# Early pairs of a SwiGLU: the weight sum a21 + a22 from two transfers on GpSimd's queue instead of a VectorE addition

## The chip, the cores and the metric

The kernel runs on one core of one Trainium2 chip. The metric is the device time of one execution in microseconds, the median of several runs.

## The reference

Two token groups (512 and 256 tokens, 768 together, width 1024) go through a two-layer encoder with shared weights. Each layer is a half SwiGLU, a mixer, and another half SwiGLU, so there are four SwiGLUs in all:

```
def swiglu(h, wg, wu, wd):
    return (jax.nn.silu(h @ wg) * (h @ wu)) @ wd

x = x + 0.5 * swiglu(rmsnorm(x, f1_n), f1_g, f1_u, f1_d)
x = x + mixer(rmsnorm(x, mix_n), ...)
x = x + 0.5 * swiglu(rmsnorm(x, f2_n), f2_g, f2_u, f2_d)
```

The hidden width is 2816, all data are float32. The mixer of the first layer is a spatial gating unit beside windowed attention; that of the second is neighbourhood attention. A last RMSNorm follows.

## The kernel before

**Arithmetic.** A float32 product is made of three products of rounded operands: each operand is split into a rounded part and a remainder (`wsplit`, lines 112 to 124: ScalarE casts the weights to `whi`, line 122, and VectorE subtracts to get `wlo`, line 123), and TensorE multiplies hi x hi, lo x hi and hi x lo (`mm3`, line 188).

**Seven products for eight.** The hidden width is cut into 11 pairs of 128-column tiles. In one pair, the weights of gate (and likewise of up) are a 2 x 2 matrix of blocks of 512 x 128: a11 and a12 (first tile, upper and lower half of the 1024 rows), a21 and a22 (second tile). The activations are cut in two halves of 384 tokens and two halves of the width. Each 2 x 2 block product is done by Winograd's scheme with seven block products in place of eight. They need weight combinations, made by `sums` (line 725) into tiles of 128 x 512 in the work pool (tag "s", a ring of eight):

- s1 = a21 + a22 (for the product with activations t1)
- s2 = s1 - a11 (for t2)
- s3 = a11 - a21 (for t3)
- s4 = a12 - s2 (for b22), in place of s2

All of these are VectorE instructions on line 727. A weight tile of 128 columns and 1024 rows is one transfer of 512 KB by SyncE's queue (`raw`, line 99) into a ring of four buffers.

**Early pairs.** The first four pairs of each SwiGLU (`EARLY`) run in two parts. First, in an order written out by hand (`ORDERS`, line 699; twelve steps, three per pair), only the products with b11 and b21 and the first hidden quarter are made; they need just a11 and a12, and the other activations are not ready yet. Later each of the four pairs loads its two tiles again (`entry`, line 641) and makes the other five products for gate and up, ten in all (`settle`, line 645), in the order t2, t3, n4, t1, b22. In `settle` the weights of the next product are prepared by `parts` (line 546) while the current one runs; the t2 weights of the next pair's gate are prepared at the end of the current pair, for pairs 1 and 2. While a pair settles, VectorE also makes the operands for the down projection of the pair before (`operands`, line 492). After pair 2 the down projection of pairs 0 and 1 runs (`down`, line 747), and so on for each two pairs.

**Order.** TensorE's order is as the program emits it. The other engines' order is made ahead by the framework's scheduler, which may bring instructions forward, transfers above all, when their buffers are free; on the chip each queue then runs strictly in order. In the second and fourth SwiGLU, those after a mixer, GpSimd makes the remainders `wlo` of the b11 weights of pairs 1 to 3; otherwise it has nothing to do near the early pairs.

`raw` has one more duty: from the 20th weight transfer on, each call also issues one small copy that builds tables for the second mixer on SyncE's queue (`spare`).

Of the kernel before, what the change touches and what calls it, by code (L numbers as in the profile page):

```python
# [9 lines left out]
F32 = mybir.dt.float32  # L10
# [4 lines left out]
ALU = mybir.AluOpType  # L15

P = 128
D = 1024
KD = D // P
FF = 2816  # L20
# [24 lines left out]
EARLY = 4  # L45
ORDERS = (0, 1, 0, 1, 2, 2, 0, 1, 3, 2, 3, 3), (0, 1, 0, 1, 0, 2, 1, 3, 2, 3, 2, 3)

WTOTAL = 12 * D * FF + 8 * EARLY * P * D + D * 1792 + 2 * D * D + D * 3072 + D * 512
VTOK = (4.0,9.0)
GAP0 = 5.2  # L50
SGU = (8.0, 3.0, 4.0)
# [4 lines left out]
class Trunk:  # L56
# [39 lines left out]
        return side  # L96


    def raw(self, name, k0, nk, c0, n, raw=None, eng=None):
        i = len(self.units)  # L100
        self.units.append((name, k0, nk, c0, n))
        size = P * nk * n
        src = self.aps["w"][self.woff : self.woff + size].rearrange("(p f) -> p f", p=P)
        self.woff += size
        if raw is None:
            raw = self.rawp.tile([P, nk * n], F32, tag="raw", name=f"raw{i}")
        (eng or self.nc.sync).dma_start(raw, src)
        if self.spare and i >= 20:
            self.spare.pop(0)()
        return raw.rearrange("p (k n) -> p k n", k=nk)  # L110
# [367 lines left out]
    def ffn(self, pre):  # L478
        nc = self.nc
# [3 lines left out]
        mixed = bool(self.unfed)  # L483
# [37 lines left out]
            yield sub(h21, h21, h11)  # L521
            yield put("n4", h21)

        entries, entered = {}, {}

        def pair(p):

# [2 lines left out]
            names = ("gate", "up")  # L530
            a = {}

            def load(tiles):
                for n in names:
                    for i in tiles:
                        r = self.first.pop(0) if self.first else self.raw(f"{pre}_w_{n}", 0, KD, (2 * p + i) * P, P)
                        a[n, i + 1, 1], a[n, i + 1, 2] = r[:, 0:4, :], r[:, 4:8, :]

            h = hs[p] = {}
            s, bank, e = {}, {}, {}  # L540
# [5 lines left out]
            def parts(n, b):  # L546
                name = {"t2": "s2", "t3": "s3", "t1": "s1", "b22": "s4"}.get(b)
                with self.tc.high_priority() if b == "t2" and p == urgent else nullcontext():
                    return self.wsplit(sums(n, name) if name else a[n, 2, 2], nc.vector)

            def product(n, w, b, key, start, st=None):
                if start:
                    mm = key == "Y" or key == "X" and p != EARLY - (1 if mixed else 2)
                    bank[key, n] = (self.psum() if mm else self.psum(self.aux, "aux"))[:, :H]
                self.run_until(lambda: b in self.made)
                with ExitStack() as stack:
                    if early and b in ("b11", "b21"):
                        stack.enter_context(self.tc.high_priority())
                    if early and not fresh and b in ("b11", "b21"):
                        if len(order) >= NW and order[-NW]:  # L560
                            stack.enter_context(self.tc.issue_after(order[-NW]))
                        order.append(None)
                    st = st or self.wsplit(w, nc.gpsimd if early and mixed and p and b == "b11" else nc.vector)
                for k in range(4):
                    self.mm3(
                        bank[key, n], (st[0][:, k, :], st[1][:, k, :]), self.b[b][k], start and k == 0, k == 3, not start
                    )

            def keep(out, key, n):

                e[n, out] = etile(out)
                nc.scalar.copy(e[n, out], bank[key, n])  # L572
                next(steps, None)
# [6 lines left out]
            def hidden(i, half, g, u):  # L580

                self.run_until(lambda: half in scales)
                h[i, half] = t = g if half else etile("sg")
                v = u if half else etile("v")
                r = rt[:, HALVES[half][0] : HALVES[half][1]]
                nc.vector.tensor_tensor(out=t, in0=g, in1=r, op=ALU.mult)  # L586
                nc.scalar.activation(t, t, AF.Silu)
                self.freed = nc.vector.tensor_tensor(out=v, in0=u, in1=r, op=ALU.mult).ins
                nc.vector.scalar_tensor_tensor(out=t, in0=t, scalar=0.5, in1=v, op0=ALU.mult, op1=ALU.mult)  # L589

            def begin(n, p1):

                bank["Y", n] = self.psum()[:, :H]
                nc.scalar.copy(bank["Y", n], p1)
# [40 lines left out]
            def p3():  # L635
# [2 lines left out]
                    add("Z", n, "u2")  # L638
                hidden(0, 1, e["gate", "u2"], e["up", "u2"])

            def entry():
                load((0, 1))
                return parts("gate", "t2")

            def settle(st):

                todo = [(n, b) for b in ("t2", "t3", "n4", "t1", "b22") for n in names]
                key = {"t1": "Z", "b22": "Z"}
                for i, (n, b) in enumerate(todo):
                    now, st = st, None  # L650
                    if i + 1 < len(todo):
                        st = parts(*todo[i + 1])
                    elif p + 1 < EARLY and (p % 2 or not p):
                        entered[p + 1] = entries[p + 1]()
                    if b == "t2":
                        begin(n, e[n, "p1"])
                    product(n, None, b, key.get(b, "Y"), b == "t1", now)
                    if b in ("t2", "t3"):
                        keep(b.replace("t", "u"), "Y", n)
                    elif b == "n4":  # L660
                        next(steps, None)
                    else:
                        add("Z", n, "u3" if b == "t1" else "u2")
                    if n == "up":
                        if b == "n4":
                            hidden(1, 0, bank["Y", "gate"], bank["Y", "up"])
                        elif b == "t1":
                            hidden(1, 1, e["gate", "u3"], e["up", "u3"])
                        elif b == "b22":
                            hidden(0, 1, e["gate", "u2"], e["up", "u2"])  # L670

            if early:
                entries[p] = entry
                load((0,))
                p1()
                yield
                p2()
                yield
                with self.tc.high_priority():
                    hidden(0, 0, bank["X", "gate"], bank["X", "up"])  # L680
                self.hids.append(self.freed)
                yield
# [5 lines left out]
                steps = operands(p - 1) if p < NPAIR - 1 else self.last_operands(dl, 0, hs[p - 1], acc)  # L688

            if early:  # L690
                settle(now)
            else:
                for f in (p1, p6, p2, p7, p4, p5, p3) if p == NPAIR - 1 else (p1, p6, p2, p7, p5, p3, p4):
                    f()
            for _ in steps:
                pass

        stages = [pair(p) for p in range(NPAIR)]
        for p in ORDERS[mixed]:
            next(stages[p])  # L700
        for p in range(NPAIR):
            for _ in stages[p]:
                pass
            if p == 2:
                acc += [self.fw.tile([P, H], F32, tag=f"p1{j}", name=f"p1{j}") for j in range(4)]
            if p and p % 2 == 0 and p < NPAIR - 1:
                self.down(pre, range(p - 2, p), d, acc)
            if p == NPAIR - 2:
                self.down(pre, range(p - 1, p), d, acc)
# [15 lines left out]
    def sums(self, a11, a12, a21, a22, s, n, name):  # L725

        f = lambda o, x, y, op: self.nc.vector.tensor_tensor(out=o, in0=x, in1=y, op=op)  # L727
        if name == "s1":
            return s[n, "s1"]
        if name == "s4":  # L730
            t = s[n, "s2"]
            f(t, a12, t, ALU.subtract)
            return t
        if name == "s2":
            t = s[n, "s1"] = self.fw.tile([P, 4, P], F32, tag="s", name="s1", bufs=8)
            f(t, a21, a22, ALU.add)
        t = s[n, name] = self.fw.tile([P, 4, P], F32, tag="s", name=name, bufs=8)
        if name == "s3":
            f(t, a11, a21, ALU.subtract)
        else:  # L740
            f(t, s[n, "s1"], a11, ALU.subtract)
        return t
# [989 lines left out]
def trace(nc, phases=PHASES):  # L1732
# [4 lines left out]
    inp("xt", (T // P, P, D))  # L1737
    inp("w", (WTOTAL,))
    inp("gains", (P, KD * len(NORMS)))
# [18 lines left out]
def layout(units, i):  # L1758
    x = np.concatenate([i["x_prompt"][0], i["x_sample"][0]], axis=0)
    w = np.zeros(WTOTAL, np.float32)  # L1760
    off = 0
# [44 lines left out]
```

## Time and profile before

| | us |
|---|---|
| median of 3 runs | 2600.09 (2599.57 to 2600.18) |
| span of the profiled execution | 2599.3 |
| TensorE busy in it | 2557.6 |
| VectorE busy | 2250.6 |
| ScalarE busy | 1364.7 |
| GpSimd busy | 113.4 |

The four SwiGLUs lie at about 0 to 500, 720 to 1240, 1240 to 1740 and 2050 to 2600 us; their early pairs take roughly the first 150 us of each. The table's busy times are sums over the whole span. TensorE's row has the same share nearly everywhere, so the places where it falls short have to be looked for in the timeline. In a timeline row the first number is the start, the second the duration; a bracket at its end gives the idle time of that engine just before the instruction and what ended it.

### The profile page before, as it was taken

The numbers are of one execution on the slowest core, as the hardware profiler recorded it, in microseconds if no ns is written. First come the engines' busy times: TensorE is split into PE (matmuls) and PEld (weight loads), VectorE is DVE, ScalarE is ACT, GpSimd is POOL, SyncE is SP. The second block draws the span as 40 slices with busy tenths as digits, with TensorE's granted clock in tenths as the row PEclk, the third lists the DMA queues.
The fourth block names the chain that finished last, engine by engine and source line by source line (L and its number), as shares of the span: only waits on it lengthen the run. The fifth ranks groups of instructions, "written<-read, shape, count | busy, mean of one in ns | idle before, by whom it ended". The sixth has DMA issues, their size and how long they took to land.

```text
span 2599.3 us, 41191 instructions
## 1 busy us (share of the span) xinstructions
PE 2557.6 (98%) x15114; PEld 2489.5 (96%) x15114; DVE 2250.6 (87%) x4691; ACT 1364.7 (53%) x2869; POOL 113.4 (4%) x191
## 2 busy tenths in 40 slices
PE   8999999999999999999999999999999999999998
PEld 8999999988899999999999999998898999999997
DVE  7998898889779989889999889886777699888897
ACT  7554454556656544445655445454545475444543
POOL 0000000000120000000000000001222210000000
PEclk9999999999999999999999999999999999999999
DMA  6333222421133322223222222242221332222222
GB/s 217 112 106 101 71 82 66 139 84 51 55 106 98 98 66 74 74 65 98 84 95 79 68 76 71 65 145 64 64 64 40 106 98 90 82 68 79 69 67 77
DMA packets 86202, 221.88 MB, mean 85 GB/s; under 512 B 20464, under 2 KB 33264, under 8 KB 86000
## 3 DMA queue, kind: packets, MB, share of 16 engines
q1 hardware_dynamic: 85712, 218.96, 26.9%
q8 instruction: 119, 1.95, 0.3%
q14 instruction: 83, 0.68, 0.1%
q10 hardware_dynamic: 288, 0.29, 0.0%
HBM read 209.78 MB, written 15.07 MB: 87 GB/s over the span
## 4 chain that ended last, share of the span: by engine, by line
PE 66%; DVE 5%; ACT 1%; issue 1%; DMA 1%; DVEq 0%; ACTq 0%; SPq 0%
PE ps_mm L152 40%; PE ps_aux L152 25%; PE ps_aux L156 1%; DVE wlo L123 1%; DMA raw<-in_w 1%; ACT p L1089 0%; DVE tmp L415 0%; DVE p L1099 0%; DVE p L1083 0%; DVE s L727 0%; DMA mf<-in_nmask 0%; DVE u L589 0%; DVE u L577 0%; DVE acc L235 0%; DVE tmp L393 0%
## 5 line engine op out<-in xcount | busy, mean ns | idle before, releaser
L122 ACT CAST whi<-s 128x512 fp32r<-128x512 f32 x496 | 304.9, 621 | 404.7 <-DVE s L727 178.6
L122 ACT CAST whi<-raw 128x512 fp32r<-128x512 f32 x504 | 305.4, 619 | 215.6 <-PE ps_mm L152 87.5
L123 DVE TENSOR_TENSOR wlo<-s,whi 128x512 fp32r<-128x512 f32 x496 | 338.3, 686 | 53.3 <-ACT whi L122 48.2
L123 DVE TENSOR_TENSOR wlo<-raw,whi 128x512 fp32r<-128x512 f32 x468 | 320.7, 693 | 15.2 <-ACT whi L122 11.3
L152 PE MATMUL ps_mm<-db,whi 128*128 128x384 f32 x864 | 219.3, 334 | 0.4 <-DVE sg L586 0.4
L152 PE MATMUL ps_aux<-dt,whi 128*128 128x384 f32 x864 | 219.2, 334 | 0.0
L152 PEld LDWEIGHTS ps_mm<-db,whi 128*128 128x128 f32 x864 | 155.9, 188 | 0.8 <-DVE sg L586 0.8
L152 PEld LDWEIGHTS ps_aux<-dt,whi 128*128 128x128 f32 x864 | 156.0, 188 | 0.0
L152 PE MATMUL ps_mm<-xh,whi 128*128 128x512 f32 (+1 forms) x416 | 146.2, 352 | 0.0
L152 PE MATMUL ps_aux<-dt,wlo 128*128 128x384 f32 x432 | 144.4, 334 | 1.4 <-DVE wlo L123 1.4
L152 PE MATMUL ps_mm<-db,wlo 128*128 128x384 f32 x432 | 144.3, 334 | 0.0
L152 PE MATMUL ps_mm<-xl,whi 128*128 128x512 f32 (+1 forms) x416 | 141.4, 340 | 0.0
L152 PE MATMUL ps_mm<-xh,wlo 128*128 128x512 f32 (+1 forms) x416 | 141.2, 339 | 0.0
L727 DVE TENSOR_TENSOR s<-raw 128x512 f32<-128x512 f32 x124 | 85.0, 687 | 20.9 <-DMA raw<-in_w 20.9
L577 DVE TENSOR_TENSOR u<-ps_aux,u 128x384 f32<-128x384 f32 x176 | 97.3, 553 | 5.6 <-PE ps_aux L152 5.2
L727 DVE TENSOR_TENSOR s<-raw,raw 128x512 f32<-128x512 f32 x124 | 84.2, 687 | 20.4 <-DMA raw<-in_w 20.2
L152 PE MATMUL ps_aux<-dh,whi 128*128 128x384 f32 x384 | 97.5, 334 | 0.0
L779 DVE TENSOR_TENSOR x<-ps_aux,x 128x384 f32<-128x384 f32 x160 | 84.9, 552 | 13.6 <-PE ps_aux L152 13.6
L1089 ACT ACTIVATE p<-p,st 128x256 f32<-128x256 f32 (+3 forms) x144 | 68.9, 480 | 49.4 <-DVE st L1087 49.3
L572 ACT COPY u<-ps_mm 128x384 f32<-128x384 f32 x176 | 83.5, 475 | 16.7 <-PE ps_mm L152 16.6
L779 DVE TENSOR_TENSOR x<-ps_mm,x 128x384 f32<-128x384 f32 x160 | 86.4, 552 | 5.8 <-PE ps_mm L152 5.5
L152 PEld LDWEIGHTS ps_mm<-xh,whi 128*128 128x128 f32 x416 | 79.8, 192 | 9.3 <-issue 0.9
(515 smaller groups left out, 8088.5 us busy)
## 6 DMA issues: line engine op xcount, KB each, us to landing
raw<-in_w SPq DMA_DIRECT2D x346, 512.0 KB, 3.7
xdm<-x SPq DMA_DIRECT2D x16, 384.0 KB, 2.4
x<-in_x SPq DMA_DIRECT2D x16, 192.0 KB, 4.6
tok<-in_xt SPq DMA_DIRECT2D x12, 256.0 KB, 5.2
xold<-xdm SPq DMA_DIRECT2D x8, 384.0 KB, 3.1
x<-xdm SPq DMA_DIRECT2D x8, 384.0 KB, 4.6
out_y<-y SPq DMA_DIRECT2D x8, 384.0 KB, 2.7
tab<-skew SPq DMA_DIRECT2D x8, 256.0 KB, 6.3
```

The lines of the kernel that those rows point to most:

```text
L122: nc.scalar.copy(hi, src)
L123: (eng or nc.gpsimd).tensor_tensor(out=lo, in0=src, in1=hi.bitcast(F32), op=ALU.subtract)
L152: self.nc.tensor.matmul(out, lhsT=lhsT, rhs=rhs, start=start, stop=stop, **kw)
L156: self.nc.tensor.transpose(out, src, self.ident)
L572: nc.scalar.copy(e[n, out], bank[key, n])
L577: nc.vector.tensor_tensor(out=t, in0=bank[key, n], in1=t, op=ALU.add)
L727: f = lambda o, x, y, op: self.nc.vector.tensor_tensor(out=o, in0=x, in1=y, op=op)
L779: nc.vector.tensor_tensor(out=o, in0=ps, in1=o, op=ALU.add)
L1089: ins = nc.scalar.activation(outs[i], outs[i], AF.Exp, bias=nm[:, i : i + 1], accum_out=sm[:, i : i + 1])
```

## The change

In the early pairs, s1 = a21 + a22 is no longer an addition on VectorE. A new function `added` of a pair, for gate and for up, issues two transfers of 256 KB from memory by GpSimd's queue into the s1 tile: a22 plainly, then a21 with an adding write onto it. For that the two blocks are laid out twice more in the weight array, which grows by 4 x 4 x 4 blocks of 256 KB (16.8 MB). `added` of pair 0 is called after the ninth of the twelve early steps; that of pair p + 1 at the start of the settling of pair p. `sums` then makes s2 alone for these pairs. The raw tiles are loaded as before, since s3, s4 and n4 need a21 and a22 as well. The later seven pairs and the down projection are as before.

```diff
-WTOTAL = 12 * D * FF + 8 * EARLY * P * D + D * 1792 + 2 * D * D + D * 3072 + D * 512
+WTOTAL = 12 * D * FF + 16 * EARLY * P * D + D * 1792 + 2 * D * D + D * 3072 + D * 512
...
-    def raw(self, name, k0, nk, c0, n, raw=None, eng=None):
+    def raw(self, name, k0, nk, c0, n, raw=None, eng=None, **kw):
...
-        (eng or self.nc.sync).dma_start(raw, src)
+        (eng or self.nc.sync).dma_start(raw, src, **kw)
...
+            def added():
+                for n in names:
+                    t = s[n, "s1"] = self.fw.tile([P, 4, P], F32, tag="s", name="s1", bufs=8)
+                    for k, kw in ((4, {}), (0, {"accum_op": ALU.add})):
+                        self.raw(f"{pre}_w_{n}", k, 4, (2 * p + 1) * P, P, t.rearrange("p a b -> p (a b)"), nc.gpsimd, **kw)
...
             if early:
-                entries[p] = entry
+                entries[p], addeds[p] = entry, added
...
             if early:
+                if p + 1 < EARLY:
+                    addeds[p + 1]()
                 settle(now)
...
-        for p in ORDERS[mixed]:
+        for i, p in enumerate(ORDERS[mixed]):
             next(stages[p])
+            if i == 8:
+                addeds[0]()
...
+        if name == "s2" and (n, "s1") in s:
+            t = s[n, "s2"] = self.fw.tile([P, 4, P], F32, tag="s", name="s2", bufs=8)
+            f(t, s[n, "s1"], a11, ALU.subtract)
+            return t
```

More of the change, by code (lines that the diff above doesn't have):

```diff
@@ L522, in operands_2 @@
             yield put("n4", h21)
-        entries, entered = {}, {}
+        entries, entered, addeds = {}, {}, {}
         def pair(p):
```

## The prediction

> **What bounds the kernel now.** I read the page first: its engine row and its groups for what the change removes.
>
> ```profile
> PE 2557.6 (98%) x15114; PEld 2489.5 (96%) x15114; DVE 2250.6 (87%) x4691; ACT 1364.7 (53%) x2869; POOL 113.4 (4%) x191
> L727 DVE TENSOR_TENSOR s<-raw 128x512 f32<-128x512 f32 x124 | 85.0, 687 | 20.9 <-DMA raw<-in_w 20.9
> q1 hardware_dynamic: 85712, 218.96, 26.9%
> q10 hardware_dynamic: 288, 0.29, 0.0%
> ```
>
> TensorE (PE) is busy 98% of 2599.3 us, so a faster VectorE (DVE) pays only where PE stands still. The second row is the instruction in question, a21 + a22, 124 times; the change drops 32 of them (4 SwiGLUs, 4 early pairs, gate and up). No queue of GpSimd (POOL) appears: q1 and q10 are SP's and ACT's.
>
> Next the busy time by stretches: two early pairs of the second SwiGLU, what follows them, and one stretch of the third SwiGLU's early pairs.
>
> ```profile
> 804.50:827.40 22.90, 21.85 (x123) 21.00 (x123) 22.67 (x49) 11.87 (x25) 0.00 (x0) 1.00 0.28 92
> 827.40:849.80 22.40, 21.39 (x121) 20.75 (x121) 22.29 (x43) 11.75 (x25) 0.00 (x0) 1.00 0.28 95
> 849.80:900.00 50.20, 50.20 (x290) 50.20 (x291) 45.89 (x84) 25.32 (x51) 0.00 (x0) 1.00 0.30 95
> 1300.00:1320.00 20.00, 20.00 (x116) 20.00 (x117) 19.27 (x35) 10.52 (x21) 0.00 (x0) 1.00 0.37 125
> ```
>
> The columns are length, then PE, PEld, DVE, ACT and POOL busy, granted clock, DMA share and GB/s. In the first two DVE is busy all but 0.23 and 0.11 us, and PE misses about 1 us of each. From 849.8 on PE misses nothing. In the third SwiGLU PE misses nothing even among the early pairs, so relief there is worth nothing.
>
> Then PE's timeline, for every idle piece in the early pairs of the first and second SwiGLU, and the first and the last of six in the fourth (idle 0.95, 0.33, 0.25, 0.79, 0.21, 0.79: a copy of the second).
>
> ```profile
> 54.99 0.45 PE L152 MATMUL ps_mm<-t30h,whi 128*128 128x384 f32 x1 [2.23 <-ACT whi L122]
> 56.28 0.44 PE L152 MATMUL ps_mm<-t30h,wlo 128*128 128x384 f32 x1 [0.68 <-DVE wlo L123]
> 78.73 0.44 PE L152 MATMUL ps_mm<-t20h,whi 128*128 128x384 f32 x1 [1.88 <-ACT whi L122]
> 79.69 0.44 PE L152 MATMUL ps_mm<-t20h,wlo 128*128 128x384 f32 x1 [0.36 <-DVE wlo L123]
> 103.31 0.44 PE L152 MATMUL ps_mm<-t20h,wlo 128*128 128x384 f32 x1 [0.79 <-DVE wlo L123]
> 154.18 0.44 PE L152 MATMUL ps_mm<-t20h,wlo 128*128 128x384 f32 x1 [0.45 <-DVE wlo L123]
> 803.46 0.44 PE L152 MATMUL ps_mm<-t20h,whi 128*128 128x384 f32 x1 [0.95 <-ACT whi L122]
> 804.42 0.45 PE L152 MATMUL ps_mm<-t20h,wlo 128*128 128x384 f32 x1 [0.34 <-DVE wlo L123]
> 807.04 0.44 PE L152 MATMUL ps_mm<-t30h,wlo 128*128 128x384 f32 x1 [0.26 <-DVE wlo L123]
> 827.34 0.45 PE L152 MATMUL ps_mm<-t20h,wlo 128*128 128x384 f32 x1 [0.79 <-DVE wlo L123]
> 848.28 0.44 PE L152 MATMUL ps_mm<-t20h,whi 128*128 128x384 f32 x1 [0.21 <-ACT whi L122]
> 849.70 0.44 PE L152 MATMUL ps_mm<-t20h,wlo 128*128 128x384 f32 x1 [0.80 <-DVE wlo L123]
> ...
> 2130.59 0.45 PE L152 MATMUL ps_mm<-t20h,whi 128*128 128x384 f32 x1 [0.95 <-ACT whi L122]
> ...
> 2176.84 0.44 PE L152 MATMUL ps_mm<-t20h,wlo 128*128 128x384 f32 x1 [0.79 <-DVE wlo L123]
> ```
>
> Nearly all stand before t2, whose weight is s2 = a21 + a22 - a11: the sum, the difference, ACT's rounding (whi), the rest (wlo). Idle sums: 6.39 us in the first SwiGLU, 3.35 in the second, 3.32 in the fourth. Two in the first cost more:
>
> ```profile
> 56.00:64.00 8.00, 7.71 (x35) 7.72 (x36) 6.70 (x18) 4.13 (x10) 0.00 (x0) 0.79 0.39 128
> 78.00:86.00 8.00, 6.92 (x29) 6.61 (x30) 7.49 (x13) 4.49 (x9) 0.00 (x0) 0.79 0.27 70
> ```
>
> After the stops of 2.23 and 1.88 us the granted clock is 0.79 over 8 us, or 0.21 x 8 = 1.7 us lost each time; after the stops under 1 us of the later SwiGLUs it stays at 1.00 (rows above).
>
> **What goes.** DVE's timeline around the stall at 803-804, and three rows for later use:
>
> ```profile
> 800.25 0.69 DVE L727 TENSOR_TENSOR s<-raw 128x512 f32<-128x512 f32 x1
> 800.86 0.16 DVE L327 TENSOR_TENSOR sm<-sm 128x3 f32<-128x3 f32 x1
> ...
> 801.99 0.69 DVE L727 TENSOR_TENSOR s<-s,raw 128x512 f32<-128x512 f32 x1
> ...
> 74.80 0.56 DVE L577 TENSOR_TENSOR u<-ps_aux,u 128x384 f32<-128x384 f32 x1 [0.29 <-PE ps_aux L152]
> ...
> 76.21 0.68 DVE L727 TENSOR_TENSOR s<-raw 128x512 f32<-128x512 f32 x1
> ...
> 824.46 0.68 DVE L727 TENSOR_TENSOR s<-s,raw 128x512 f32<-128x512 f32 x1
> ```
>
> The sum takes 0.69 us but the next instruction starts 0.61 us later, so two sums per pair free 1.2 us of DVE. Where DVE is full, everything behind comes 1.2 us earlier, up to the stall. Second SwiGLU: pair 0 of 1.55 us: 1.2; pair 1: 0.79, all; pair 2: 1.01, all: 3.0. Fourth: 1.2 + 0.79 + 1.0 = 3.0. First: pair 0 of 2.91: 1.2; pair 1 of 2.24: 1.2 (2.24 at most, since its second sum stands late in DVE's order, at 76.21); pair 2: 0.79; pair 3: 0.45: 3.6. Of the two half-clock stretches I count one as gone, 1.7 (none to two, 0 to 3.4), since both stops shrink to about 1 us. Third: 0. Together 11.3 us. What is late next is the same chain without its first link, with DVE still nearly full; the residue (0.35 in the second, 1.7 and 1.0 in the first) stays.
>
> **What comes.** Per early pair four transfers of 256 KB on POOL's queue. No row shows POOL issuing one, nor an accumulating one. Nearest rows:
>
> ```profile
> raw<-in_w SPq DMA_DIRECT2D x8, 256.0 KB, 3.4
> first<-in_w SPq DMA_DIRECT2D x7, 256.0 KB, 5.0
> 59.33 0.34 SPq L107 DMA_DIRECT2D raw<-in_w  x1
> 782.88 1.30 POOL L123 TENSOR_TENSOR wlo<-raw,whi 128x512 fp32r<-128x512 f32 x1 [2.09 <-ACT whi L122]
> L123 POOL TENSOR_TENSOR wlo<-raw,whi 128x512 fp32r<-128x512 f32 x36 | 48.7, 1361 | 833.2 <-ACT whi L122 826.1 <-DVE st L1083 5.2 <-PE ps_mm L152 1.9
> ```
>
> Landing of a plain one: 3.4 us (5.0 in the full start). Accumulating: from 3.4 to four times that, 13.6 us; I take 5, near the plain row, for one more read. Issue: between SP's 0.34 and a POOL pass over such a tile, 1.30; I take 0.8. The accumulate must wait for the plain one, and POOL waits in order, so gate plain, gate accumulating, up plain, up accumulating end 3.4 + 3.4 + 5 + 4 x 0.8 = 15 us after the start. The Trainium skill (DMA: Bandwidth & Descriptors, Two DMAs through the same engine are not ordered) asks for just that wait on the first one's semaphore; no run here shows it yet.
>
> For pairs 1 to 3 the lead is about a pair, over 22 us: hidden, with 7 us to spare. For pair 0 POOL is free at 782.88 + 1.30 = 784.2, so the up sum is there at 799 against the 800.9 at which DVE now has it; if issued at 1.3 it is 801. In the fourth SwiGLU the same. I take off one of the two pair-0 gains, 1.2 (from 0 to 2.4). What is queued behind POOL's waits: its remainders of b11 if transfers slip between them; the last is that row, so I cost that at 0.
>
> The start of the kernel is where added bytes hurt:
>
> ```profile
> 25.00:30.00 5.00, 4.46 (x25) 4.46 (x26) 2.53 (x10) 5.00 (x15) 0.00 (x0) 1.00 1.03 402
> ...
> 17.90 2.42 SPq L107 DMA_DIRECT2D raw<-in_w  x4
> ...
> raw<-in_w SPq DMA_DIRECT2D x8, 512.0 KB, 5.4
> ...
> 28.43 2.70 ACT L122 CAST whi<-raw 128x512 fp32r<-128x512 f32 x5
> ```
>
> DMA engines first, then SP's issue of pairs 2 and 3's weights, their landing and ACT's use of them. The DMA engines are full up to here. Pair 0's 1.05 MB takes 1.05/402 = 2.6 us of them; ACT's in-order rounding of weights at 28-31 us follows loads issued at 18-20 us that land in 5.4 us, so 2 to 3 us of slack cover most. I take 0.7 lost (0 to 2.6). SP gets no added load; the bias-table copies tied to its load counter move earlier into time when it waits for buffers: 0. The ring of eight weight-sum tiles is now filled (two pairs' sums, two differences, two s3): 0, at most the 0.6 of a delayed DVE pass per pair.
>
> **Sum.** 11.3 - 1.2 - 0.7 = 9.4 us, against 2600.09 (median; the profiled span is 2599.3, the 0.8 around it is kept): **2590.7 us**.
>
> **Rivals.** (1) The stalls hang on DVE's fixed order rather than its load. For: in pair 1 of the first SwiGLU the second sum came at 76.21, after DVE had paused 0.29 us for PE at 74.80. Then half of 9.6 goes, no half-clock stretch, less 1.0 for the start: 3.8 us, 2596.3. Chance 0.21.
>
> (2) Slower: the accumulating transfer is slow, A us. DVE takes its instructions in order, so a late sum stops DVE and then PE. In pair 0 of the second and fourth SwiGLU the sum becomes late from A = 801.99 - 784.18 - 6.8 - 3.2 = 7.8; pair 1's up sum, asked for when pair 0 settles at about 800 and used at 824.46, only from 24.5 - 10 = 14.5, and so the other pairs. At A = 13.6 the two pairs 0 cost 2 x 5.8 = 11.6 while the others gain 11.3 - 2.4 - 0.7 = 8.2: 2603.5; it turns slower from A = 11.9, and beyond 14.5 every pair pays. Against it: the plain 3.4. Chance 0.10.
>
> (3) DVE keeps POOL from writing descriptors. With DVE idle 0.23 us of 22.9, transfers would run only once DVE itself stops for them: 6.8 to 13.6 us for each of 16 pairs, 2700 or more. The Trainium skill (SBUF — State Buffer, Who interferes with whom) says that an exclusive port pair lets DVE's 2-port copies and casts block POOL's descriptor writing, but not two-input tensor_tensor, which is nearly all DVE does here. The trace agrees as far as it goes: POOL's own passes, beside a busy DVE, take 1.36 us in the mean against 1.30 for the one above. Chance 0.03.
>
> (4) The added 1.05 MB per 22 us, 47 GB/s on 92 to 125, makes the other weights late: each is waited for already (20.9 us in the second row), mostly while PE has work. About 6 us lost, 2606. Chance 0.06.
>
> (5) More than forecast: all idle pieces and both half-clock stretches go, 13.1 + 3.4 = 16.5: 2583.6. Chance 0.10. The forecast holds 0.50, with a range of its own of 2586 to 2596.
>
> **Numbers.** 0.2% (5.2 us) is about what can be told from no change. Faster: 0.46 of the forecast and rival 5's 0.10, 0.56. Same: rival 1, 0.04 of the forecast, 0.02 of rival 2: 0.27. Slower: 0.08 + 0.03 + 0.06 = 0.17. The range 2583 to 2606 leaves out rival 3 and the far parts of 2 and 4.
>
> **What would show it.** Right: 92 sums from raw instead of 124; a POOL queue with 64 transfers of 256 KB; the idle pieces at 78, 103, 827, 849 and their copies in the fourth SwiGLU gone; at most one half-clock stretch before 100 us; PE unchanged in the third. Wrong: DVE waiting for the accumulated tile; stalls before t2 of the old size (rival 1); landing above 8 us (rival 2); a later first matmul of pair 2 at the start.

## The result, and the profile after

The changed kernel takes 2593.33 us (median of 19 runs, 2591.56 to 2598.13) against 2600.18 for the kernel before on the same chips (19 runs): a ratio of 0.9976, 95% interval 0.9970 to 0.9982. It is 6.85 us faster; 9.4 were forecast, 2590.7.

The page of the changed kernel first, the engines, GpSimd's queue, SyncE's weight loads and GpSimd's transfers; then the sum's row in the groups by line and the issue instruction in the view of line 107:

```profile
PE 2556.4 (98%) x15114; PEld 2491.2 (96%) x15114; DVE 2232.9 (86%) x4659; ACT 1365.6 (53%) x2869; POOL 159.7 (6%) x255
q0 software_dynamic: 7168, 16.78, 3.0%
raw<-in_w SPq DMA_DIRECT2D x346, 512.0 KB, 3.7
s<-in_w POOLq DMA_DIRECT2D x64, 256.0 KB, 4.9
```

```profile
L737 DVE TENSOR_TENSOR s<-raw 128x512 f32<-128x512 f32 x92 | 63.0, 685 | 12.3 <-DMA raw<-in_w 12.0
```

```profile
L107 POOL DMA_DIRECT2D s<-in_w x64: 546/856/1223, 5.9 to 2164.3; - x64
DMA to landing us min/median/max: 2.8/4.9/8.3
```

The change does what it says: 92 sums on VectorE instead of 124, and 64 transfers of 256 KB on a queue that wasn't there. An issue takes GpSimd 0.86 us, a transfer lands 4.9 us after it. VectorE is 17.7 us less busy. TensorE's timeline in the first SwiGLU (start, duration, and in brackets the idle time before it):

```profile
25.66 0.44 PE L152 MATMUL ps_mm<-b210h,whi 128*128 128x384 f32 x1 [2.51 <-ACT p L602]
...
54.80 0.44 PE L152 MATMUL ps_mm<-t30h,whi 128*128 128x384 f32 x1 [0.42 <-ACT whi L122]
...
78.75 0.44 PE L152 MATMUL ps_mm<-t30h,wlo 128*128 128x384 f32 x1 [0.35 <-DVE wlo L123]
...
120.80 1.01 PE L152 MATMUL ps_aux<-dt,whi 128*128 128x384 f32 x2 [4.42 <-ACT whi L122]
...
122.86 1.01 PE L152 MATMUL ps_aux<-dt,whi 128*128 128x384 f32 x2 [0.64 <-ACT whi L122]
```

The stop of 2.23 us is down to 0.42. The one of 1.88 us before t2 of pair 1 is gone and 0.35 us is left before its t3, and those at 79.69, 103.31 and 154.18 are gone. In the second and the fourth SwiGLU one stop of 0.54 us, before t3 of pair 0, is left of the six that the prediction lists. But two others have come in the first: 2.51 us in the start, where the kernel before stopped for 0.70, and 4.42 us at 120.80, the first product of the down projection of pairs 0 and 1, where the kernel before stopped for nothing. The second one runs on at half clock, as the stretch from 118 to 128 us shows (columns as in the prediction: PE, PEld, DVE, ACT, POOL, granted clock, DMA share, GB/s):

```profile
118.00:128.00 10.00, 6.37 (x17) 5.23 (x18) 8.24 (x14) 3.76 (x7) 0.00 (x0) 0.53 0.20 57
```

TensorE runs the same 15114 matmuls in every kernel here, in the same order but for a few neighbours in the first mixer that change places, so two traces can be laid side by side matmul by matmul. The table gives, for the first matmul that the kernel before starts at or after the time on the left, how much later (+) or earlier (-) the other kernel starts it. The columns are the changed kernel, a second profile of it (e9), and experiments that follow.

```
before us   after      e9      e1      e4      e8      e7     e10
       28     1.5     0.4     0.5    -0.8    -0.3     0.3    -0.4
       54    -0.2    -1.3    -1.2    -2.6    -2.1    -1.5     0.4
       86    -4.6    -5.7    -5.6    -6.9    -6.4    -5.8     0.3
      120    -5.6    -6.7    -6.6    -7.9    -7.4    -6.8     0.3
      125     3.6     2.5    -6.6    -7.9     0.8    -6.8     0.3
      330     1.1     0.1    -9.3   -10.6    -1.9    -9.5     0.3
      780     4.0    -1.5    -9.6    -9.0    -0.5    -6.0     3.5
      900     1.3    -5.3   -12.6   -12.8    -4.4   -10.1     7.0
     1240     1.3    -5.3   -12.6   -12.8    -4.4   -10.1     7.0
     1400     0.1    -6.5   -13.9   -14.0    -5.6   -11.4    11.0
     2095    -0.1    -6.9   -14.3   -14.4    -5.8   -11.2    10.7
     2250    -3.7   -10.9   -17.9   -17.8    -9.0   -12.1    15.0
     2599    -3.7   -10.9   -17.9   -17.8    -8.9   -12.1    15.1
```

Read downwards, "after" gains 5.6 us until 120, loses 9.2 within the next 5, and leaves the first SwiGLU 1.1 us behind. It gains 2.7 between 780 and 900 (second SwiGLU) and 3.6 between 2095 and 2250 (fourth). What lies between 330 and 780 holds the first mixer: same instructions, but from -1.6 to +3.5 from profile to profile. That goes with half clock: between 500 and 720 us the clock records add up to 3.4 us of it in e9, 10.2 in the kernel before, 13.7 in the changed kernel and 17.1 in e7. So a single profile tells a SwiGLU's gain to about 1 us (2.7 and 3.8 for the second in the two profiles of the change), and the whole to some 3 us.

Why does TensorE stop at 120.80? VectorE's timeline there, and SyncE's (first the changed kernel's two, then the kernel before's):

```profile
110.18 0.56 DVE L577 TENSOR_TENSOR u<-ps_aux,u 128x384 f32<-128x384 f32 x1 [2.94 <-PE ps_aux L152]
...
116.42 0.56 DVE L577 TENSOR_TENSOR u<-ps_aux,u 128x384 f32<-128x384 f32 x1 [0.93 <-PE ps_aux L152]
...
118.86 0.56 DVE L496 TENSOR_TENSOR sg<-sg 128x384 f32<-128x384 f32 x1
119.34 0.68 DVE L737 TENSOR_TENSOR s<-raw,raw 128x512 f32<-128x512 f32 x1
120.06 0.69 DVE L737 TENSOR_TENSOR s<-s,raw 128x512 f32<-128x512 f32 x1
```

```profile
101.44 0.33 SPq L107 DMA_DIRECT2D raw<-in_w  x1
101.81 0.53 SPq L1633 DMA_DIRECT2D tab<-skew  x1
102.44 0.54 SPq L107 DMA_DIRECT2D raw<-in_w  x1
103.02 0.53 SPq L1633 DMA_DIRECT2D tab<-skew  x1
104.31 0.33 SPq L107 DMA_DIRECT2D raw<-in_w  x1
104.69 0.53 SPq L1633 DMA_DIRECT2D tab<-skew  x1
105.39 0.57 SPq L107 DMA_DIRECT2D raw<-in_w  x1
```

```profile
112.70 0.69 DVE L727 TENSOR_TENSOR s<-raw,raw 128x512 f32<-128x512 f32 x1
```

```profile
106.03 2.74 SPq L107 DMA_DIRECT2D raw<-in_w  x4
108.82 1.86 SPq L1619 DMA_DIRECT2D tab<-skew  x3
```

The down projection's first sum is made at 119.34, behind the whole last part of pair 2's settling, though VectorE stood idle for 2.94 us before 110.18 and the two loads that the sum waits for, issued at 101.44 and 102.44, had landed at 105.06 and 107.97. The kernel before made it at 112.70, ahead of that part. So the sum is neither late by load nor by its data: it stands late in VectorE's fixed order. What changed upstream is SyncE's queue: a bias-table copy stands between each two of the four loads, which stood together before. `raw` issues one such copy per call from the 20th weight transfer on, and `added` calls `raw` too, so the copies come earlier in the program, in between these loads. How the scheduler got from there to the late place of the sum isn't recorded; whether the copies are the cause can be tried.

### The profile page after: what moved, and what is told of

The parts are those of the page before. It is cut to its first block, busy times and chain, and to the rows that moved or that the text cites. A ratio compares the mean times of both kernels' runs of the same rounds, so it can differ in the third digit from the quotient of the medians.

```text
span 2595.6 us, 41312 instructions
## 1 busy us (share of the span) xinstructions
PE 2556.4 (98%) x15114; PEld 2491.2 (96%) x15114; DVE 2232.9 (86%) x4659; ACT 1365.6 (53%) x2869; POOL 159.7 (6%) x255
## 4 chain that ended last, share of the span: by engine, by line
PE 68%; DVE 4%; ACT 1%; issue 1%; DMA 0%; DVEq 0%; ACTq 0%
PE ps_mm L152 41%; PE ps_aux L152 25%; PE ps_aux L156 1%; DVE wlo L123 0%; DVE tmp L415 0%; ACT p L1103 0%; DVE p L1113 0%; DVE p L1097 0%; DMA raw<-in_w 0%; ACT whi L122 0%; DVE tl L209 0%; DVE qk L1577 0%; DVE sg L589 0%; ACT diag L306 0%; DVE v L588 0%
## 5 line engine op out<-in xcount | busy, mean ns | idle before, releaser
L123 DVE TENSOR_TENSOR wlo<-raw,whi 128x512 fp32r<-128x512 f32 x468 | 319.9, 692 | 17.4 <-ACT whi L122 14.2
L123 POOL TENSOR_TENSOR wlo<-raw,whi 128x512 fp32r<-128x512 f32 x36 | 48.5, 1355 | 746.0 <-ACT whi L122 738.1
```

The lines of the kernel that those rows point to most:

```text
L123: (eng or nc.gpsimd).tensor_tensor(out=lo, in0=src, in1=hi.bitcast(F32), op=ALU.subtract)
```

## The experiments

| kernel | median us (range, runs) | ratio to before, 95% |
|---|---|---|
| the change | 2593.33 (2591.56 to 2598.13, 19) | 0.9976 (0.9970 to 0.9982) |
| e1: copies as before | 2586.56 (2582.52 to 2588.54, 5) | 0.9946 (0.9932 to 0.9959) |
| e2: pair 0 of the first SwiGLU as before | 2598.08 (2592.33 to 2601.14, 11) | 0.9985 (0.9977 to 0.9994) |
| e3: second and fourth SwiGLU alone | 2595.74 (2591.79 to 2597.37, 11) | 0.9980 (0.9971 to 0.9989) |
| e4: e1 and late transfers at the start | 2584.00 (2581.45 to 2585.50, 5) | 0.9937 (0.9924 to 0.9949) |
| e5: e4, VectorE makes the sums once more | 2612.31 (2611.00 to 2612.71, and one of 6499.12; 5) | 1.0045 (1.0031 to 1.0059) |
| e6: e4, plain transfers alone | 2582.99 (2582.19 to 2583.98, 5) | 0.9934 (0.9921 to 0.9946) |
| e7: e4 without the third SwiGLU | 2585.04 (2584.57 to 2589.09, 5) | 0.9942 (0.9928 to 0.9955) |
| e8: the change, late transfers at the start | 2592.75 (2592.24 to 2593.41, 6) | 0.9971 (0.9960 to 0.9982) |
| e9: the change again | 2593.65 (2590.28 to 2599.36, 10) | 0.9975 (0.9966 to 0.9985) |
| e10: e5 again | 2612.10 (2608.26 to 2616.97, 3) | 1.0047 (1.0030 to 1.0065) |
| e11: e4, first SwiGLU alone | 2592.35 (2589.68 to 2594.37, 7) | 0.9968 (0.9957 to 0.9979) |

**The copies (e1).** GpSimd's calls are taken out of the count:

```diff
+        self.sums_on_pool = 0
...
-        if self.spare and i >= 20:
+        late = eng is self.nc.gpsimd and i >= 20
+        self.sums_on_pool += late
+        if self.spare and not late and i - self.sums_on_pool >= 20:
```

> GpSimd's weight-sum transfers no longer advance the count that issues SyncE's bias-table copies, so the loads of the first down projection stand together again in SyncE's queue. Theory A (the new 4.42 us stop of TensorE at 120.80, before down of pairs 0 and 1 in the first SwiGLU, comes from those copies standing between down's loads): the stop falls under 0.6 us and the half-clock stretch behind it goes, 4 to 9 us off the changed kernel's 2593.3, so 2584 to 2589. Theory B (the two sums of pair 3 hold two of the eight weight-sum tiles, and down's own sums have to wait for them): stop and time stay, 2592 to 2594.5.

Measured: 2586.56, 6.8 us below the changed kernel. SyncE and VectorE in its timeline, then the stretch in which the changed kernel fell to half clock:

```profile
100.42 4.28 SPq L108 DMA_DIRECT2D raw<-in_w  x4
104.75 1.18 SPq L1636 DMA_DIRECT2D tab<-skew  x2
```

```profile
106.14 0.68 DVE L740 TENSOR_TENSOR s<-raw,raw 128x512 f32<-128x512 f32 x1
```

```profile
118.00:128.00 10.00, 10.00 (x59) 10.00 (x58) 9.87 (x20) 7.61 (x17) 0.00 (x0) 1.00 0.51 157
```

The loads stand together, the sum is made at 106.14, TensorE misses nothing and the clock stays at 1.00. Theory A holds and B falls: the eight tiles are as crowded here as in the changed kernel.

**The start (e2, e4, e8, e9).** In e2 pair 0 of the first SwiGLU keeps its sums on VectorE; in e8 its transfers are only asked for later, and e4 is e8 with e1's copies. (The edit calls `added` of pair 0 three steps later in the other SwiGLUs as well. In the second they still go out at the same place: in e4 the last two of pair 0 from 759.42, in the changed kernel from 772.18, where its TensorE is 13 us behind e4's.)

```diff
# e2
-            if i == 8:
+            if i == 8 and pre != 'l0_ffn1':
# e4, e8
-            if i == 8:
-                addeds[0]()
+            if i == 11:
+                with self.tc.issue_after(self.hids[-2]) if pre == 'l0_ffn1' else nullcontext():
+                    addeds[0]()
```

> Pair 0 of the first SwiGLU makes its sums on VectorE as before; all other early pairs as in the changed kernel. Theory C (those 1.05 MB in the full start cost the 2.51 us stop at 25.66 us and a half-clock stretch after it, more than the 1.2 us of VectorE that they free): the stop is back at 0.7 us, the stretch at 26 us is gone, 1.8 + 1.7 - 1.2 = 2.3 us off 2593.3, 2591 (2589.5 to 2592). If the start is no matter (the forecast's 0.7 lost against 1.2 won): 2593.8. The stop at 120.80 stays under both.

> As the first run here, and in the first SwiGLU pair 0's four transfers are asked for only after the hidden values of pair 2, when the start's rush of loads is over. Theories A and C together: stops at 25.66 and 120.80 both small, 2582 to 2588. If only A holds, as the first run. If only C holds, 2590 to 2592. If pair 0's sums now come too late, TensorE stops before t2 of pair 0 at about 54 us for more than the 0.42 and 0.56 us of the changed kernel.

> The changed kernel, with only the four transfers of pair 0 in the first SwiGLU asked for later; the bias-table copies as in the changed kernel. If the stop at 25.66 us is made by those transfers in the full start: it is back at 0.7, without the half-clock stretch behind it, 1.8 + 1.7 = 3.5 us off 2593.3: 2590 (2588 to 2591.5); the stop of 4.42 us at 120.80 stays, since the copies still stand between the loads of down. If the start doesn't matter: 2593. If the copies don't make the stop at 120.80, it goes here too and the time is near 2584.

> The changed kernel itself, for a second profile of it. Its times lie in two groups (13 of 19 from 2591.6 to 2593.7, 6 from 2595.9 to 2598.1) and the profile at hand, with the 2.51 us stop at 25.66 and a half-clock stretch after it, is of the upper one. If that stop makes the upper group, a profile near 2592 shows it under 1.5 us and without the stretch, and one near 2597 shows both again. The 4.42 us stop before down of pairs 0 and 1 is there in either.

In e8 the stop at 25 us is back at 0.70 and the one before down is still there, as theories A and C have it:

```profile
25.26 0.44 PE L152 MATMUL ps_mm<-b210h,whi 128*128 128x384 f32 x1 [0.70 <-ACT p L602]
...
118.97 1.01 PE L152 MATMUL ps_aux<-dt,whi 128*128 128x384 f32 x2 [4.42 <-ACT whi L122]
```

But its time, 2592.75, is only 0.6 us below the changed kernel's, not 3.5: a miss for theory C's price. The second profile of the changed kernel goes some way to tell why:

```profile
25.98 0.45 PE L152 MATMUL ps_mm<-b210h,whi 128*128 128x384 f32 x1 [1.31 <-ACT p L602]
...
119.69 1.01 PE L152 MATMUL ps_aux<-dt,whi 128*128 128x384 f32 x2 [4.42 <-ACT whi L122]
```

In this execution the stop in the start is 1.31 us and no half clock follows; the table's columns e9 and e8 stand 0.7 apart at 120 us. So the 2.51 us of the first profile are not there each time. The runs of e8 lie within 1.2 us, those of the changed kernel within 6.6 and 9.1, but it isn't shown that the start spreads them: of the 7.1 us between the two profiles' spans (2595.6 and 2588.5) only 1.1 are there at 120 us, and 4.5 come between 330 and 780. e4 gives 2584.0, the best time here of a kernel that makes all its sums: 16.7 us below the 2600.73 of the kernel before in that set. Its range overlaps that of e1, so what the late transfers add to e1 is not settled. Its first SwiGLU has this left:

```profile
24.70 0.45 PE L155 MATMUL ps_mm<-b210h,whi 128*128 128x384 f32 x1 [0.70 <-ACT p L605]
...
52.38 0.44 PE L155 MATMUL ps_mm<-t30h,whi 128*128 128x384 f32 x1 [0.52 <-ACT whi L125]
53.66 0.44 PE L155 MATMUL ps_mm<-t30h,wlo 128*128 128x384 f32 x1 [0.66 <-DVE wlo L126]
...
56.75 0.45 PE L155 MATMUL ps_mm<-t30h,wlo 128*128 128x384 f32 x1 [0.60 <-DVE wlo L126]
...
76.44 0.44 PE L155 MATMUL ps_mm<-t30h,wlo 128*128 128x384 f32 x1 [0.35 <-DVE wlo L126]
```

e2 was a miss: 2598.08 for 2591. Without its transfers pair 0 has its old stop again, and another one, at the second down projection, is longer than the 1.45 us of the kernel before:

```profile
54.90 0.44 PE L152 MATMUL ps_mm<-t30h,whi 128*128 128x384 f32 x1 [2.24 <-ACT whi L122]
...
291.04 0.92 PE L152 MATMUL ps_aux<-dt,whi 128*128 128x384 f32 x2 [2.76 <-ACT whi L122]
```

Against what was expected, the stop before the first down projection didn't stay: it is 1.45 and 0.80 us in place of 4.42. Leaving out four calls of `raw` moves the copies too. The four loads of down stand together again, as in e1, and the first sum is made at 113.35:

```profile
102.06 4.28 SPq L107 DMA_DIRECT2D raw<-in_w  x4
```

So e2 changes more than the start; it speaks for theory A once more, and doesn't show what pair 0's transfers alone are worth. The profiled execution is one of e2's quickest (2592.66 us), and the 4.8 us between its median and the changed kernel's aren't explained by these rows.

**Where the gain lies (e3, e11, e7).** Each limits the calls of `added` to some SwiGLUs: e3 is the changed kernel with those after a mixer alone, e11 and e7 are e4 with the first alone and with all but the third.

```diff
# e3
-            if i == 8:
+            if i == 8 and mixed:
...
-                if p + 1 < EARLY:
+                if p + 1 < EARLY and mixed:
# e11: "and pre == 'l0_ffn1'" at both places, e7: "and pre != 'l1_ffn1'"
```

> Only the second and the fourth SwiGLU, those after a mixer, take their sums by GpSimd's queue; the first and third as before the change. By TensorE's idle time in the two profiles these two gain 2.6 and 3.6 us and the first loses about 1: 2600.1 - 6.2 = 2593.9 (2592.5 to 2595). If the gain comes from all four as forecast (3.0 and 3.0 less 1.2 here, 4.6 in the first), this gives 2600.1 - 4.8 = 2595.3 at best and is slower than the changed kernel by what the first gains.

> As the run with late transfers and copies as before (2584.0), but only the first SwiGLU takes its sums by GpSimd's queue. If the gains of the four SwiGLUs add up: 16 in all, 5 in the second and fourth by the run that has these alone, about 1 in the third, so 10 in the first: 2590 (2588.5 to 2592). If the first is worth only the 3.6 and 1.7 us of the forecast: 2595.

> As the run with late transfers and copies as before (2584.0), with the third SwiGLU's early pairs making their sums on VectorE as before the change. If relief of VectorE is worth nothing where TensorE already misses nothing, as forecast: 2584 within 1.5. If the 1.3 us less of TensorE's idle time between 1240 and 1400 us in the changed kernel's profile comes from it: 2585.3.

The second and fourth alone bring 5.0 us (2600.73 - 2595.74), the 4.8 of the forecast rather than the 6.2 read from the two profiles. The first alone, without the copies' stop, brings 7.7 (2600.05 - 2592.35); 10 were expected, and the 5.3 of the forecast is too little. e7 is 1.0 slower than e4 with overlapping ranges, so its time fits both of its expectations; but in its column of the table the third SwiGLU (1240 to 1400) gains 1.3 us like the others, though it has no transfers there. So this gain doesn't come from relief in the third SwiGLU. The kernel before has one stop there, 0.45 us at 1362.29; it is gone in e7 and in e3, and still there (0.42) in e11, where the second SwiGLU is as before. The rest of the 1.3 is open. The parts add up to 12.7 of e4's 16.7 us; the 4 us between are as large as the spread of single runs, and I leave them open.

**VectorE's work (e5, e10).** On the basis of e4 VectorE makes each of the 32 sums once more; the result is overwritten at once.

```diff
             t = s[n, "s2"] = self.fw.tile([P, 4, P], F32, tag="s", name="s2", bufs=8)
+            f(t, a21, a22, ALU.add)
             f(t, s[n, "s1"], a11, ALU.subtract)
```

> As the run with late transfers and copies as before (2584.0), but VectorE makes each of the 32 sums again, into the s2 tile, and then overwrites it with the difference: VectorE's work is that of the kernel before, while the sum that is used still comes by GpSimd's queue. If VectorE's load makes the stalls, the idle pieces before t2 come back, about 9.6 us, with two half-clock stretches at 1.7 each: 2597 (2593 to 2600). If the stalls hang on when the sum is ready (the loads, the fixed order) and not on the load, 2584 to 2587.

> The kernel with the dead sums again, for its profile: 2612 instead of the 2597 that VectorE's load alone was to give. If the load does it, VectorE is busy in all but a few tenths of each early pair, the third SwiGLU's too, and the idle pieces of TensorE in the four SwiGLUs add up to some 20 us, each ended by VectorE or ScalarE. If it is the dead sum's place in the order instead, VectorE itself waits for weight loads ahead of it, by more than 1 us at a time, before the stops of TensorE.

e5 gave 2612.31 us, 28 more than e4 and 12 more than the kernel before, and neither expected time. Its profile is of the execution that took 6499 us, so e10 is the same kernel once more (2612.1, 3 runs). TensorE in e10, and the row of the kernel before that its sixth line repeats:

```profile
55.34 0.45 PE L155 MATMUL ps_mm<-t30h,whi 128*128 128x384 f32 x1 [3.00 <-ACT whi L125]
...
78.98 0.44 PE L155 MATMUL ps_mm<-t20h,whi 128*128 128x384 f32 x1 [1.88 <-ACT whi L125]
79.94 0.44 PE L155 MATMUL ps_mm<-t20h,wlo 128*128 128x384 f32 x1 [0.35 <-DVE wlo L126]
...
103.57 0.44 PE L155 MATMUL ps_mm<-t20h,wlo 128*128 128x384 f32 x1 [0.79 <-DVE wlo L126]
...
154.43 0.44 PE L155 MATMUL ps_mm<-t20h,wlo 128*128 128x384 f32 x1 [0.45 <-DVE wlo L126]
...
291.88 0.44 PE L155 MATMUL ps_aux<-dt,wlo 128*128 128x384 f32 x1 [1.45 <-DVE wlo L126]
```

```profile
291.62 0.44 PE L152 MATMUL ps_aux<-dt,wlo 128*128 128x384 f32 x1 [1.45 <-DVE wlo L123]
```

Stop by stop the first SwiGLU of the kernel before is back, to 0.01 us from 78 us on, with both half-clock stretches, and the column e10 stays at +0.3 until 330. The 3.00 us are 0.77 more than the old stop; ahead of it VectorE waits 0.81 us for a weight load, before a dead sum:

```profile
44.72 0.69 DVE L741 TENSOR_TENSOR s<-raw 128x512 f32<-128x512 f32 x1 [0.81 <-DMA raw<-in_w]
```

But for that, the gain of the first SwiGLU is VectorE's time, although the sums that are used still come from GpSimd's queue. In the second, the stops of pairs 0 and 2 are back as well (0.95, 0.33 and 0.24; 0.21 and 0.79). Elsewhere in the later SwiGLUs the dead sums cost more than the old ones, and there VectorE waits for weights; pair 1 of the second has 2.28 us for the old 0.79:

```profile
827.75 0.69 DVE L741 TENSOR_TENSOR s<-raw 128x512 f32<-128x512 f32 x1 [3.23 <-DMA raw<-in_w]
```

```profile
830.50 0.44 PE L155 MATMUL ps_mm<-t20h,wlo 128*128 128x384 f32 x1 [2.28 <-DVE wlo L126]
```

So both expectations of e10 hold, each in its place: load in the first SwiGLU and in part of the second, the dead sum's place ahead of its load in the rest.

**The accumulating transfer (e6).** On the basis of e4 only the first of the two transfers is issued, so s1 holds a22 alone:

```diff
-                    for k, kw in ((4, {}), (0, {"accum_op": ALU.add})):
+                    for k, kw in ((4, {}),):
```

> As the run with late transfers and copies as before (2584.0), with the accumulating transfer left out, so s1 holds a22 alone: 32 transfers on GpSimd's queue for 64, 8.4 MB less, and no wait of GpSimd for the first transfer. If the accumulating transfers cost time by their landing, their waits or their traffic, this is faster by 2 us or more (below 2582); if they are hidden, as the 4.9 us of landing against a lead of some 22 us says, 2584 within 1.5.

2582.99, 1.0 below e4: within the 1.5. By the landing records of the changed kernel the plain transfers took 3.6 us from the start of their issue (median of 32, 2.8 to 6.7), the accumulating ones 6.1 (3.9 to 8.3). All of it is hidden: in the changed kernel no sum landed less than 8.3 us before the difference that reads it, in e4 none but pair 0's in the first SwiGLU, asked for late, which land 1.9 and 2.9 us ahead.

## Why the prediction was right, and where not

The time came out inside the forecast's own range, but from larger sums on both sides than its 11.3 - 1.2 - 0.7. That the total is within 2.6 us of the forecast is luck in part: a gain that was counted too small and a loss that was put at nothing nearly cancel.

- **What bounds the kernel:** right. VectorE's work in the early pairs sets TensorE's stops; e10 brings them back by that work, in the first SwiGLU and in part of the second.
- **Second and fourth SwiGLU, 3.0 + 3.0 - 1.2 = 4.8:** about right. e3, which has them alone, is 5.0 faster; the profiles of the change show 2.7 and 3.6, those of e9 3.8 and 4.0. The 1.2 for a late sum was wrong. I had pair 0's transfers start when GpSimd is done with its remainders, at 784.2. They went out ahead of the last four of them, from 768.93 to 774.0, the two plain ones first and the two accumulating ones behind them, with one wait of 2.08 us. The last landed at 778.84. VectorE's first difference, which waits for the first accumulating one, is made at 801.87, 24 us after that one landed:

```profile
768.93 1.17 POOL L107 DMA_DIRECT2D s<-in_w  x2
772.18 1.81 POOL L107 DMA_DIRECT2D s<-in_w  x2 [2.08 <-DMA s<-in_w]
```

```profile
801.87 0.67 DVE L737 TENSOR_TENSOR s<-s,raw 128x512 f32<-128x512 f32 x1
```

- **Third SwiGLU, 0:** right for its own transfers, by e7's column. That TensorE misses nothing there was read from 1300 to 1320 alone and leaves out the 0.45 us at 1362.29.
- **First SwiGLU, 3.6 + 1.7:** too small. In e4, where nothing new stands in the way, the table shows 10.6 (0.8 of it in the first 28 us, before any sum). Pair 0 gains about the 1.2 that I allowed (from 2.91 to 0.52, 0.66 and 0.60), pairs 2 and 3 their 0.79 and 0.45. Pair 1 gains 1.9 (2.24 to 0.35), the 1.45 at 291.62, which I had not counted, is gone, and both half-clock stretches go, not one: 9.1 of the 9.8. The largest stop, 2.23, stands before t3, whose weight a11 - a21 has no sum in it; so "nearly all stand before t2" passes over it, and it shrank because VectorE had two sums less to make ahead of it.
- **"the bias-table copies tied to its load counter move earlier into time when it waits for buffers: 0":** this is the step that failed. The copies did move, but in between the loads of the down projection, and VectorE's order was remade around them: 9.2 us of TensorE's time in either profile of the change, 6.8 us between the medians of e1 and the change. I priced the moved transfers by the time they take on SyncE, and not by what stands behind them in the queue.
- **Start, 0.7 (0 to 2.6):** fits, though the transfers went out earlier than I had them, from 5.93 to 14.2 us. 0.7 between e9 and e8 at 120 us; 2.3 between the first profile of the change and e4 at 28 us. Whether it is the full DMA engines or the tiles that the token loads have to wait for was not separated.
- **Issue 0.8, landing 3.4 and 5:** near: 0.86, 3.6 and 6.1.
- **The rivals.** (1) falls for the first SwiGLU: with VectorE's work back the stops are back, with it gone they are gone. A late place in a fixed order was a cause all the same, at a spot I had not looked at. (2) falls: the accumulating transfer took 6.1 us in the median and 8.3 at most. Its 7.8, from which pair 0 would be late, goes by the issue at 784.2; with the real one there were 24 us. (3) falls: no issue took GpSimd more than 1.22 us. (4) falls for the change: the other weights land in 3.7 us as before. (5), all idle pieces and both stretches, at 2583.6, is what e4 reaches once the copies' stop is out (2584.0).

## What to carry to other kernels

A helper with a side effect, here a counter that feeds another queue, moves that effect with every new caller: list what each added call does besides its transfer, and ask which loads it now stands between. Where an order is made ahead, relief at one place can cost more at the next, so look for idle time of the engine just ahead of a new stop: if it was idle, and the data for the late instruction had landed, the order is at fault and not the load. Laying two traces side by side by the bound engine's instruction count shows each gain and loss at its place, also where the sum of them looks as forecast.

## What the runs showed of the hardware

A stop of TensorE can have a second price, a stretch at half clock behind it, and whether it falls due is not settled by the stop's length. In e10 a stop of 1.88 us was followed by a granted clock of 0.79 over 8 us, and one of 2.43 us by 1.00:

```profile
79.00:87.00 8.00, 7.65 (x33) 7.33 (x34) 6.94 (x13) 4.62 (x9) 1.07 (x2) 0.79 0.37 110
1340.00:1348.00 8.00, 6.83 (x39) 6.79 (x40) 8.00 (x17) 2.73 (x7) 0.00 (x0) 1.00 0.00 0
```

```profile
1341.17 0.44 PE L155 MATMUL ps_aux<-b220h,whi 128*128 128x384 f32 x1 [2.43 <-DVE u L580]
```

In the clock records of these profiles the half-clock stretches last 3.41 us or a multiple of it (6.83, 10.24), but for one at each kernel's end that runs on past its last instruction. The Trainium skill (TensorE: Matmul & The Clock Gate, Why this matters for your kernels) asks for no gaps over some 3 us between bursts of matmuls; here a stretch followed a stop of 1.88 us already.
